# A third weight block, later stores and an earlier gate in a hybrid decoder layer

## The chip, the cores and the metric

The kernel runs on one core of a Trainium2 chip. Its time is device microseconds of one execution, given as the median of several runs. A separate profiled execution supplies the trace that the text reads from.

## The reference, cut to what matters

One layer, 512 tokens of width 2048, all in float32. Two branches read the same normalised input, and their outputs are merged:

```
mod = silu(c) @ w_ada + b_ada;  shift, scale, gate = split(mod, 3)
h = rms_norm(x) * (1 + scale) + shift
proj = h @ w_in                         # all channels of both branches
a_out = swa_attention(...) * silu(ag);  y_a = a_out @ w_o_swa
o = gated_delta_rule(q, k, v, g, beta)  # 16 key heads, 32 value heads
o = rms_norm(o) * silu(dz);             y_b = o @ w_o_dn
y = sigmoid(mg_a) * y_a + sigmoid(mg_b) * y_b
out = x + gate * (y @ w_out)
```

The delta rule works on chunks of 64 tokens. Each chunk needs the inverse of a unit lower triangular 64 x 64 matrix for each head, and then a scan over the chunks carries a state of 128 x 128 per value head. `gate` is a vector of 2048 numbers, the last third of `silu(c) @ w_ada + b_ada`; it is wanted only at the very end.

## The kernel before, in words

**Matmuls.** Each float32 operand is split into a high part (a rounded copy, `whi`, made by ScalarE) and a low part (`wlo`, the difference, made by VectorE); line 50, `split`. A product is three matmuls on TensorE (PE), high by high, high by low, low by high (`mm3`, lines 239 to 244).

**Weights.** All weight matrices are a list of jobs in the order of their use (`plan`, line 158). A job is a block of 128 x 2048 numbers, 1 MB. `load_job` (197) starts its transfer on SyncE's queue (SP) into a tile `raw` of the pool `wraw`, which has two buffers. A block is split in two halves (`split_half`, 206), each into one of three buffers for `whi` and `wlo`. A channel tile (`channel_tile`, 246) takes one block, 48 matmuls of 128 x 512, and gives 128 channels for all tokens. When PE has used a half, `half_done` puts the next split on a list, `due`; when a block's second half has been split, its `raw` buffer is free and the next `load_job` is put there.

**Order.** After every second of a channel tile's 16 steps the kernel calls `pump` (81), so eight times in a tile. A pump first runs the list `due`, then moves all generators in `live` on (a generator says with `yield n` how many pumps it wants to wait), then the paced ones, then those in `side` queues (`beside`, 78), each at a rate of steps per pump. In this way work of the scans, the solves and other helpers is laid between the matmuls. The framework then orders the instructions of each engine by when they are ready and by their place in the program. `ordered` (660) and `behind` (105) add the constraint that a helper's instructions come no earlier than the matmul ahead of them in the program.

**Stages.** The startup computes h; the keys' stage the keys, their matrices and the first of two triangular solves. Then comes the heads' stage, the second half of `deltanet` (593): for each of 16 heads a channel tile of queries, two of values and two of the output gate z (`heads`, 843), two channel tiles of the merge gate behind them. The generators `queries`, `values`, `zgate` and `scan` run beside the tiles of their own head and of the next one. The second solve runs on VectorE until it is drained at head 8; its buffers are the pool `sol1`. From head 2 on `od_sums` (674) builds sums of weight blocks by transfers in DRAM (`od_m`), copies on SP's queue and accumulating ones on GpSimd's.

A scan (953) goes through four chunks. In each, ScalarE copies `vn` from PSUM, VectorE scales it to `vs`, PE multiplies it (`pd`, line 988), and ScalarE puts the outputs into `osb` (993), a single buffer. At the end `osb` is normalised, transposed and multiplied with z, and `head_sums` (1034) forms four sums of quarters and stores everything to DRAM, `oq_d`, with three transfers on SP (1044).

`branch_b` (1047) is the output product of this branch: it loads `oq_d` and multiplies it with the weights `w_od` and the sums (`od`). Beside it, at a rate of 0.17, ran `gate` (1595): it loads `w_ada_gate` in 32 pieces of 512 KB (`gw`, two buffers), adds each times a number of silu(c) to an accumulator `gate_bc` on VectorE (1612, 1614), sums over the partitions with four matmuls against ones (`pgate`, 1622), adds the bias and halves (1624, 1625), and stores the result in `gate_d`. Attention and the last product follow, and are not touched.

Of the kernel before, what the change touches and what calls it, by code (L numbers as in the profile page):

```python
# [7 lines left out]
F32 = mybir.dt.float32  # L8
# [8 lines left out]
P = 128  # L17
# [19 lines left out]
class Layer:  # L37
# [153 lines left out]
    def prime(self):  # L191
        self.job_load = self.half_split = self.half_used = 0
        self.raws, self.halves, self.due = {}, {}, []
        for _ in range(2):
            self.load_job()

    def load_job(self):
        j = self.job_load
        if j < len(self.jobs):
            src = self.jobs[j][1]  # L200
            raw = self.wraw.tile([P, 2048], F32, tag="raw", name="raw")
            self.nc.sync.dma_start(out=raw[:, : src.shape[-1]], in_=src)
            self.raws[j] = raw
            self.job_load += 1

    def split_half(self):
        n = self.half_split
        j = n // 2
        if j < len(self.jobs):
            w = self.jobs[j][1].shape[-1] // 2  # L210
            raw = self.raws[j]
            hi = self.whl.tile([P, 1024], F32R, tag="whi", name="whi")
            lo = self.whl.tile([P, 1024], F32R, tag="wlo", name="wlo")
            self.split(hi[:, :w], lo[:, :w], raw[:, (n % 2) * w : (n % 2 + 1) * w])
            self.halves[n] = (hi, lo)
            self.half_split += 1
            if n % 2:
                del self.raws[j]
                self.due.append(self.load_job)

    def half(self, name):
# [57 lines left out]
    def build(self):  # L279
        tc, nc, a = self.tc, self.nc, self.a  # L280
        with ExitStack() as es:
            self.const = es.enter_context(tc.tile_pool(name="const", bufs=1))
            self.dram = es.enter_context(tc.tile_pool(name="scratch", bufs=1, space=DRAM))
            self.dnc_es = ExitStack()
            self.dnc = self.dnc_es.enter_context(tc.tile_pool(name="dnc", bufs=1, side="right"))
            self.v_d = self.dram.tile([2, P, T], F32, name="v_d")
            self.hpool = es.enter_context(tc.tile_pool(name="h", bufs=1))
            hh = self.hh = self.hpool.tile([P, KT, T], F32R, name="hh")
            hl = self.hl = self.hpool.tile([P, KT, T], F32R, name="hl")
            self.wraw = es.enter_context(tc.tile_pool(name="wraw", bufs=2, reuse_waits="tile"))  # L290
            self.whl = es.enter_context(tc.tile_pool(name="whl", bufs=3, reuse_waits="tile"))
            self.side, self.live, self.slow = {}, [], []
            self.hold, self.keep_order = 0, False
            self.od_d = {n: self.dram.tile([8, P, 2048], F32, name=f"od_{n}") for n in ("m7", "m5", "m6", "m4")}
            self.plan()
            self.psc_es = ExitStack()
            self.psc = self.psc_es.enter_context(tc.tile_pool(name="psc", bufs=4, space=PSUM, reuse_waits="tile"))
            with ExitStack() as st:
                self.startup(st)
            if self.stop == "startup":  # L300
                return
            self.ma_d = self.dram.tile([KT, P, T], F32, name="ma_d")
            self.mb_d = self.dram.tile([KT, P, T], F32, name="mb_d")
            self.ao_d = self.dram.tile([KT, P, T], F32, name="ao_d")
            self.yb_d = self.dram.tile([KT, P, T], F32, name="yb_d")
            self.deltanet()
            self.psc_es.close()
            self.dnc_es.close()
            if self.stop == "deltanet":
                return  # L310
            self.gate_d = self.dram.tile([D], F32, name="gate_d")
            self.y_d = self.dram.tile([KT, P, T], F32, name="y_d")
            self.branch_b()
            if self.stop == "branch_b":
                return
            self.attention()
            if self.stop == "attention":
                return
            self.finish()
# [273 lines left out]
    def deltanet(self):  # L593
# [10 lines left out]
        with ExitStack() as ps:  # L604
            self.pmm = ps.enter_context(tc.tile_pool(name="pmm", bufs=2, space=PSUM, reuse_waits="tile"))
            self.ptp = ps.enter_context(tc.tile_pool(name="ptp", bufs=2, space=PSUM, reuse_waits="tile"))
            self.gwk = ps.enter_context(tc.tile_pool(name="gwk", bufs=1, reuse_waits="tile"))
            sol1 = ps.enter_context(tc.tile_pool(name="sol1", bufs=1, side="right", reuse_waits="tile"))
            with ExitStack() as sa:
                wk = sa.enter_context(tc.tile_pool(name="dnA", bufs=2, reuse_waits="tile"))  # L610
                sol0 = sa.enter_context(tc.tile_pool(name="sol0", bufs=1, reuse_waits="tile"))
# [27 lines left out]
            with ExitStack() as sb:  # L639
                wk = sb.enter_context(tc.tile_pool(name="dnB", bufs=2, reuse_waits="tile"))  # L640
                self.tt = []
                for n in range(4):
                    t = wk.tile([P, NTB, P], F32, tag=f"tt{n}", name=f"tt{n}", bufs=1)
                    nc.gpsimd.memset(t[HD:P, :, 0:HD], 0.0)
                    self.tt.append(t)
                for g in range(KH):
                    if g == 2:
                        self.beside(self.ordered(self.od_sums()), 0.13, "ws")
                    if g == 8:
                        self.drain_slow(s1)  # L650
                    self.heads(wk, g)
                for j in range(3, 5):
                    self.merge_gate("ma", j, self.ma_d)
                self.drain_live()
                self.drain("ws")

    def sum_keys(self):
        return [(s, n, i) for s in ("m7", "m5", "m6", "m4") for n in range(2) for i in range(2)]
# [294 lines left out]
    def scan(self, wk, g, k, kT, TT, qd, M, epsq, st):  # L953
# [73 lines left out]
        for e in range(2):  # L1027
# [1 line left out]
            self.transpose4(pt, lambda c: osb[:, e, c, :])  # L1029
            nc.vector.tensor_tensor(out=z[e], in0=pt, in1=z[e], op=ALU.mult)  # L1030
            yield 1
        self.head_sums(g, z, osb.rearrange("p e c i -> p (e c i)").rearrange("p (q t) -> p q t", q=4))

    def head_sums(self, g, z, s):

        nc = self.nc
        TT, STT = nc.vector.tensor_tensor, nc.vector.scalar_tensor_tensor
        lo, hi = slice(0, 256), slice(256, 512)
        TT(out=s[:, 0], in0=z[0][:, hi], in1=z[1][:, hi], op=ALU.subtract)
        STT(out=s[:, 1], in0=s[:, 0], scalar=-1.0, in1=z[0][:, lo], op0=ALU.mult, op1=ALU.subtract)  # L1040
        TT(out=s[:, 2], in0=z[0][:, lo], in1=z[0][:, hi], op=ALU.add)
        STT(out=s[:, 3], in0=s[:, 1], scalar=-1.0, in1=z[1][:, lo], op0=ALU.mult, op1=ALU.subtract)
        for q, src in ((slice(0, 1), z[0][:, lo].unsqueeze(1)), (slice(1, 3), z[1].rearrange("p (q t) -> p q t", q=2)), (slice(3, 7), s)):
            nc.sync.dma_start(out=self.oq_d[q, g // 2].rearrange("q p k t -> p q k t")[:, :, g % 2, :], in_=src)


    def branch_b(self):
        tc, nc, a = self.tc, self.nc, self.a
        with ExitStack() as es:
# [3 lines left out]
            self.gwk = es.enter_context(tc.tile_pool(name="gwkb", bufs=1, reuse_waits="tile"))  # L1053
            k1 = wk.tile([P, 2, 2, T], F32, name="k1", bufs=1)
            k5 = wk.tile([P, 2, 2, T], F32, name="k5", bufs=1)
            self.beside(self.gate(wk), 0.17, "gate")
            order = self.od_order()
            raws, parts, c = {}, {}, {}

# [42 lines left out]
            for m, (name, _, _) in enumerate(order):  # L1102
                ps = {}
                for kt in range(KT):
# [15 lines left out]
                    self.half_done()  # L1120
                    if kt % 2:
                        del parts[u]
            self.drain("gate")
            for j in range(7, 9):
                self.merge_gate("ma", j, self.ma_d)
            self.drain_live()
# [468 lines left out]
    def gate(self, wk):  # L1595

        nc, a = self.nc, self.a
        acc = wk.tile([P, D], F32, name="gate_bc", bufs=1)
        ws = {}

        def load(i):
            ws[i] = wk.tile([P, 1024], F32, tag="gw", name="gw", bufs=2)
            nc.sync.dma_start(out=ws[i], in_=a["w_ada_gate"][i // 2][:, i % 2 * 1024 : i % 2 * 1024 + 1024])

        load(0)
        load(1)
        for i in range(2 * KT):
            yield
            s = self.sc[:, i // 2 : i // 2 + 1]
            o = acc[:, i % 2 * 1024 : i % 2 * 1024 + 1024]  # L1610
            if i < 2:
                nc.vector.tensor_scalar(out=o, in0=ws.pop(i), scalar1=s, scalar2=None, op0=ALU.mult)
            else:
                nc.vector.scalar_tensor_tensor(out=o, in0=ws.pop(i), scalar=s, in1=o, op0=ALU.mult, op1=ALU.add)
            if i + 2 < 2 * KT:
                load(i + 2)
        for c in range(4):
            sl = slice(c * T, (c + 1) * T)
            b = wk.tile([P, T], F32, tag="yb", name="gb", bufs=3)
            nc.sync.dma_start(out=b, in_=a["b_gate"][sl].partition_broadcast(P))  # L1620
            ps = self.ptp.tile([P, T], F32, tag="tp", name="pgate")
            nc.tensor.matmul(ps, lhsT=self.ones, rhs=acc[:, sl], start=True, stop=True)
            yield
            nc.vector.tensor_tensor(out=acc[:, sl], in0=ps, in1=b, op=ALU.add)
            nc.vector.tensor_scalar(out=acc[:, sl], in0=acc[:, sl], scalar1=0.5, scalar2=None, op0=ALU.mult)
            nc.sync.dma_start(out=self.gate_d[sl], in_=acc[0:1, sl])


# [78 lines left out]
```

## Time and profile before

| | us |
|---|---|
| median of 3 runs | 2908.98 |
| lowest and highest run | 2906.93, 2910.56 |
| profiled execution | 2908.68 |
| its span, first to last instruction | 2906.9 |
| PE busy in the span | 2839.3 |
| VectorE (DVE) busy | 1846.5 |
| ScalarE (ACT) busy | 1141.0 |
| GpSimd (POOL) busy | 270.7 |

The heads' stage lies from about 527 to 1655 us, the output product from there to about 2000. In the profile's lists a line such as `PE pd L988 <- DVE vs L980: 15.7, 6, 6.6` says that PE, at line 988 with output `pd`, waited for `vs` of VectorE: the total, how often, and the longest. In a timeline a line begins with its start and its duration, and ends in brackets with the engine's idle time before it and what ended that.

### The profile page before, as it was taken

What the parts mean: (1) busy time and instruction counts of PE and PEld (TensorE: products, weight loads), DVE (VectorE), ACT (ScalarE), POOL (GpSimd) and SP (SyncE); (2) the same over time, 40 slices, a digit from 0 to 9 for tenths busy, and PEclk for the clock granted to TensorE, in tenths of its full rate; (3) what the DMA queues carried; (4) which work ended last, traced back from release to release, by engine and by line L of the source; (5) the groups of instructions that cost most, each with busy time, mean ns of one, the idle gap of its engine ahead of it and who ended that gap; (6) DMA issues with size and microseconds to landing.
All of it is one profiled execution on the core that took longest, in us unless ns stands there. A gap on an engine that the chain in (4) does not pass through costs nothing. (4 is left out here: it accounts for less than half of the span.)

```text
span 2906.9 us, 38230 instructions
## 1 busy us (share of the span) xinstructions
PE 2839.3 (98%) x14428; PEld 2325.5 (80%) x14428; DVE 1846.5 (64%) x3020; ACT 1141.0 (39%) x2161; POOL 270.7 (9%) x266
## 2 busy tenths in 40 slices
PE   8899999999999999999999999999999999999999
PEld 6677888888887888888878888778887788788777
DVE  6765898777776655545545477765655655554565
ACT  4354333433334333333333355443344434432343
POOL 0022211101111111111110000000100100000010
PEclk9999999999999999999999999999999999999999
DMA  9747454646667767666663499876645647365575
GB/s 388 285 148 212 161 183 144 205 130 202 202 187 217 234 178 220 200 204 188 208 168 121 135 337 327 305 257 207 215 155 162 171 142 223 113 239 177 179 236 153
DMA packets 205472, 590.08 MB, mean 203 GB/s; under 512 B 74564, under 2 KB 99652, under 8 KB 154088
## 3 DMA queue, kind: packets, MB, share of 16 engines
q1 hardware_dynamic: 195080, 529.44, 53.2%
q0 software_dynamic: 10208, 58.20, 10.1%
q8 instruction: 113, 1.85, 0.3%
q14 instruction: 71, 0.58, 0.1%
HBM read 523.79 MB, written 166.40 MB: 237 GB/s over the span
## 5 line engine op out<-in xcount | busy, mean ns | idle before, releaser
L242 PE MATMUL mm<-hh,whi 128*128 128x512 f32 x2784 | 1133.2, 407 | 2.5 <-ACT whi L52 1.6
L244 PE MATMUL mm<-hh,wlo 128*128 128x512 f32 x2784 | 1090.8, 392 | 1.5 <-DVE wlo L53 1.5
L243 PE MATMUL mm<-hl,whi 128*128 128x512 f32 x2784 | 1089.1, 391 | 0.0
L53 DVE TENSOR_TENSOR wlo<-raw,whi 128x1024 fp32r<-128x1024 f32 (+1 forms) x476 | 585.5, 1233 | 457.7 <-ACT whi L52 447.9
L52 ACT CAST whi<-raw 128x1024 fp32r<-128x1024 f32 (+1 forms) x476 | 494.8, 1043 | 815.2 <-PE mm L243 644.9
L244 PEld LDWEIGHTS mm<-hh,wlo 128*128 128x128 f32 x2784 | 523.7, 188 | 116.1 <-DVE wlo L53 2.4
L242 PEld LDWEIGHTS mm<-hh,whi 128*128 128x128 f32 x2784 | 524.9, 189 | 112.7 <-issue 8.6
L243 PEld LDWEIGHTS mm<-hl,whi 128*128 128x128 f32 x2784 | 525.4, 189 | 98.5 <-issue 0.5
L243 PE MATMUL od<-wlo,oh 128*128 128x512 f32 x448 | 175.7, 392 | 3.3 <-DVE wlo L53 3.2
L242 PE MATMUL od<-whi,oh 128*128 128x512 f32 x448 | 176.4, 396 | 0.2 <-ACT whi L52 0.2
L244 PE MATMUL od<-whi,ol 128*128 128x512 f32 x448 | 175.2, 391 | 0.0
L920 POOL TENSOR_TENSOR qe<-qe,yq 128x512 f32<-128x512 f32 x32 | 47.8, 1508 | 884.3 <-DMA qe<-eg_rows 761.3
L769 POOL TENSOR_TENSOR E<-E,neg_g 128x512 f32<-128x512 f32 x64 | 80.0, 1250 | 489.4 <-DMA E<-g_rows 400.3
L819 DVE TENSOR_TENSOR A<-A,atmp 128x62 f32<-128x62 f32 (+30 forms) x124 | 111.4, 898 | 1.5
L812 DVE TENSOR_TENSOR atmp<-A 128x62 f32<-128x62 f32 (+30 forms) x124 | 110.1, 888 | 1.4
L243 PEld LDWEIGHTS od<-wlo,oh 128*128 128x128 f32 x448 | 84.6, 189 | 23.0 <-DVE wlo L53 4.9
L242 PEld LDWEIGHTS od<-whi,oh 128*128 128x128 f32 x448 | 84.4, 188 | 18.6 <-issue 1.0
L244 PEld LDWEIGHTS od<-whi,ol 128*128 128x128 f32 x448 | 84.5, 189 | 17.7
L53 DVE TENSOR_TENSOR wlo<-raww,whi 128x1024 fp32r<-128x1024 f32 x56 | 68.2, 1221 | 41.2 <-ACT whi L52 41.2
L52 ACT CAST whi<-raww 128x1024 fp32r<-128x1024 f32 x56 | 59.0, 1054 | 76.6 <-PE m L244 67.1
L966 DVE SCALAR_TENSOR_TENSOR r<-pp,neg_eg,vt 128x128 f32<-128x128 f32 x96 | 29.2, 346 | 81.0 <-PE pp L963 79.7
L1369 ACT ACTIVATE sm<-sm,mx,rs 128x256 f32<-128x256 f32 (+1 forms) x128 | 71.7, 561 | 3.3 <-DVE mx L1364 3.3
(341 smaller groups left out, 3254.2 us busy)
## 6 DMA issues: line engine op xcount, KB each, us to landing
raw<-in_w_ch SPq DMA_DIRECT2D x158, 1024.0 KB
wa<-in_w_ada_ss SPq DMA_DIRECT2D x32, 1024.0 KB
od_m<-in_w_od POOLq DMA_DIRECT2D x32, 1024.0 KB, 14.1
raw<-od_m SPq DMA_DIRECT2D x32, 1024.0 KB
raw<-in_w_od SPq DMA_DIRECT2D x24, 1024.0 KB
E<-g_rows SPq DMA_DIRECT2D x64, 256.0 KB
od_m<-in_w_od SPq DMA_DIRECT2D x16, 1024.0 KB
od_m<-od_m SPq DMA_DIRECT2D x16, 1024.0 KB
```

The costliest lines, as they stand in the source:

```text
L52: self.nc.scalar.copy(out=hi, in_=src)
L53: self.nc.vector.tensor_tensor(out=lo, in0=src, in1=hi.bitcast(F32), op=ALU.subtract)
L242: nc.tensor.matmul(ps, lhsT=wh, rhs=xh, start=first, stop=False)
L243: nc.tensor.matmul(ps, lhsT=wh, rhs=xl, start=False, stop=False)
L244: self.last_mm = nc.tensor.matmul(ps, lhsT=wl, rhs=xh, start=False, stop=last).ins
L769: nc.gpsimd.tensor_tensor(out=E, in0=E, in1=ng, op=ALU.add)
L812: eng.tensor_tensor(out=t, in0=A[:, m : m + 1, m + 1 :].to_broadcast([P, m, n]), in1=A[:, :m, m : m + 1].to_broadcast([P, m, n]), op=ALU.mult,
L819: eng.tensor_tensor(out=A[:, :m, m + 1 :], in0=A[:, :m, m + 1 :], in1=t, op=ALU.add)
L920: nc.gpsimd.tensor_tensor(out=qf, in0=qf, in1=q, op=ALU.mult)
L966: nc.vector.scalar_tensor_tensor(out=r[:, e, :], in0=pp[:, e, :], scalar=self.neg_eg[:, c, 2 * g + e : 2 * g + e + 1], in1=v[e][:, c, :], ...
L1369: nc.scalar.activation(t, t, AF.Exp, scale=r[:, h : h + 1], bias=mx[:, h : h + 1], accum_out=den[:, h : h + 1])
```

## The change

Three edits.

1. **A third weight block.** In the heads' stage a pool `wmore` gives one more buffer for `raw`, and one `load_job` more is called at the stage's start. From then on three blocks are on their way or waiting instead of two. `load_job` takes the buffer that is free, in `wraw` or in `wmore`. With the last head `wmore` is set to None, so that the extra block is used up and not loaded again.
2. **Stores.** `head_sums` becomes a generator that waits four pumps between its sums and its three stores.
3. **The gate.** It runs no longer in `branch_b` but from head 8 of the heads' stage on, in a pool `late` in the place of the second solve's `sol1`, at a rate of 0.125, under `ordered`. Its bias tile has a buffer of its own. A `yield` is added between the eviction of each of the four sums and its store. `gate_d` is made earlier, since it is written earlier.

```diff
     def load_job(self):
         j = self.job_load
-        if j < len(self.jobs):
+        pool = self.wmore if sum(p is self.wraw for p in self.raw_in.values()) == 2 else self.wraw
+        if j < len(self.jobs) and pool:
             src = self.jobs[j][1]
-            raw = self.wraw.tile([P, 2048], F32, tag="raw", name="raw")
+            raw = pool.tile([P, 2048], F32, tag="raw", name="raw")
+            self.raw_in[j] = pool
...
             if n % 2:
-                del self.raws[j]
+                del self.raws[j], self.raw_in[j]
                 self.due.append(self.load_job)
...
+                self.wmore = sb.enter_context(tc.tile_pool(name="wmore", bufs=1, reuse_waits="tile"))
+                self.load_job()
                 for g in range(KH):
+                    if g == KH - 1:
+                        self.wmore = None
...
                     if g == 8:
                         self.drain_slow(s1)
+                        es1.close()
+                        late = ps.enter_context(tc.tile_pool(name="late", bufs=1, side="right", reuse_waits="tile"))
+                        self.beside(self.ordered(self.gate(late)), 0.125, "gate")
...
                 self.drain("ws")
+                self.drain("gate")
...
         STT(out=s[:, 3], in0=s[:, 1], scalar=-1.0, in1=z[1][:, lo], op0=ALU.mult, op1=ALU.subtract)
+        yield 4
         for q, src in ((slice(0, 1), z[0][:, lo].unsqueeze(1)), (slice(1, 3), z[1].rearrange("p (q t) -> p q t", q=2)), (slice(3, 7), s)):
             nc.sync.dma_start(out=self.oq_d[q, g // 2].rearrange("q p k t -> p q k t")[:, :, g % 2, :], in_=src)
...
-            self.beside(self.gate(wk), 0.17, "gate")
...
-            self.drain("gate")
...
             nc.tensor.matmul(ps, lhsT=self.ones, rhs=acc[:, sl], start=True, stop=True)
             yield
             nc.vector.tensor_tensor(out=acc[:, sl], in0=ps, in1=b, op=ALU.add)
             nc.vector.tensor_scalar(out=acc[:, sl], in0=acc[:, sl], scalar1=0.5, scalar2=None, op0=ALU.mult)
+            yield
             nc.sync.dma_start(out=self.gate_d[sl], in_=acc[0:1, sl])
```

More of the change, by code (lines that the diff above doesn't have):

```diff
@@ L193, in prime @@
         self.raws, self.halves, self.due = {}, {}, []
+        self.raw_in, self.wmore = {}, None
         for _ in range(2):
@@ L305, in build @@
             self.yb_d = self.dram.tile([KT, P, T], F32, name="yb_d")
+            self.gate_d = self.dram.tile([D], F32, name="gate_d")
             self.deltanet()
@@ L310, in build @@
                 return
-            self.gate_d = self.dram.tile([D], F32, name="gate_d")
             self.y_d = self.dram.tile([KT, P, T], F32, name="y_d")
@@ L607, in deltanet @@
             self.gwk = ps.enter_context(tc.tile_pool(name="gwk", bufs=1, reuse_waits="tile"))
-            sol1 = ps.enter_context(tc.tile_pool(name="sol1", bufs=1, side="right", reuse_waits="tile"))
+            es1 = ExitStack()
+            sol1 = es1.enter_context(tc.tile_pool(name="sol1", bufs=1, side="right", reuse_waits="tile"))
             with ExitStack() as sa:
@@ L1031, in scan @@
             yield 1
-        self.head_sums(g, z, osb.rearrange("p e c i -> p (e c i)").rearrange("p (q t) -> p q t", q=4))
+        yield from self.head_sums(g, z, osb.rearrange("p e c i -> p (e c i)").rearrange("p (q t) -> p q t", q=4))
     def head_sums(self, g, z, s):
@@ L1618, in gate @@
             sl = slice(c * T, (c + 1) * T)
-            b = wk.tile([P, T], F32, tag="yb", name="gb", bufs=3)
+            b = wk.tile([P, T], F32, tag="gb", name="gb", bufs=1)
             nc.sync.dma_start(out=b, in_=a["b_gate"][sl].partition_broadcast(P))
```

## The prediction, made before the result was known

> **What bounds the kernel now.** I read the page first, then the chain of waits engine by engine (PE alone, by stage), then the busy times of stretches around each stall, and last the timeline of the longest stall.
>
> ```profile
> span 2906.9 us, 38230 instructions
> PE 2839.3 (98%) x14428; PEld 2325.5 (80%) x14428; DVE 1846.5 (64%) x3020; ACT 1141.0 (39%) x2161; POOL 270.7 (9%) x266
> ```
>
> TensorE is busy 2839.3 of 2906.9 us, so an edit that leaves the matmuls alone can only win from the other 67.6 us and from time at a lower clock. The change touches two stages, the heads' stage (527 to 1655 us) and the output product behind it (1655 to about 2000). PE's waits in the first, and in the second:
>
> ```profile
> PE pd L988 <- DVE vs L980: 15.7, 6, 6.6
> PE pto L276 <- DVE osb L1023: 1.3, 1, 1.3
> PE pv L973 <- ACT vt L870: 1.1, 1, 1.1
> PE ptv L276 <- DVE yv L590: 0.7, 1, 0.7
> ```
>
> ```profile
> PE od L243 <- DVE wlo L53: 3.2, 2, 2.2
> ```
>
> One wait is nearly all of it: `pd`, a matmul of the scan, waits for `vs` on VectorE six times, 15.7 us in all. Around these stalls the clock drops as well (columns: stretch, its length, busy time of PE, PEld, DVE, ACT and POOL with instruction counts, granted clock, DMA share, GB/s):
>
> ```profile
> 918.00:928.00 10.00, 6.62 (x24) 5.40 (x24) 5.25 (x12) 7.58 (x14) 0.00 (x0) 0.83 0.79 247
> 1260.00:1270.00 10.00, 8.01 (x37) 6.38 (x36) 4.39 (x8) 4.34 (x10) 0.00 (x0) 1.00 0.94 313
> 1330.00:1342.00 12.00, 9.65 (x37) 7.66 (x37) 4.38 (x8) 4.34 (x10) 0.00 (x0) 0.86 0.94 302
> 1487.50:1494.00 6.50, 6.50 (x25) 5.62 (x25) 1.14 (x3) 1.35 (x6) 0.00 (x0) 0.67 0.00 0
> 1852.00:1864.00 12.00, 9.77 (x36) 7.62 (x35) 11.57 (x14) 4.65 (x5) 0.00 (x0) 0.86 0.86 315
> ```
>
> Clock lost is length times (1 - granted): 1.7 us at 918, 1.7 at 1330, 2.1 behind the stall that ended at 1487.5, 1.7 at 1852; none at 1260. That is 5.5 us in the heads' stage and 1.7 in the output product.
>
> Why `vs` is late is told by the longest stall (start, duration, engine, line, operation, idle time before it and who ended it):
>
> ```profile
> 1460.89 12.44 SPq L202 DMA_DIRECT2D raw<-in_w_ch  x2
> 1484.74 1.04 ACT L52 CAST whi<-raw 128x1024 fp32r<-128x1024 f32 x1 [11.93 <-DMA raw<-in_w_ch]
> 1485.69 0.37 ACT L975 COPY vn<-pv 128x256 f32<-128x256 f32 x1
> 1485.82 1.23 DVE L53 TENSOR_TENSOR wlo<-raw,whi 128x1024 fp32r<-128x1024 f32 x1 [10.23 <-ACT whi L52]
> 1486.96 0.48 DVE L980 TENSOR_SCALAR vs<-vn,kd 128x128 f32<-128x128 f32 x2
> 1487.49 1.22 PE L988 MATMUL pd<-vs,k 128*128 128x256 f32 x2 [6.60 <-DVE vs L980]
> ```
>
> ScalarE stands 11.93 us at the split of a weight block that was asked for at 1460.89 and came 23.9 us later. The scan's `vn` is queued behind that split, VectorE's `wlo` and `vs` behind it too, and PE waits at `pd`. The reader is to see that a weight load nobody on PE needs yet holds two in-order engines. It happens seven times:
>
> ```profile
> L52 ACT CAST whi<-raw x164: 1030/1047/1067, 531.3 to 1648.8; 128x1024 fp32r<-128x1024 f32 x164
>   DMA raw<-in_w_ch: 41.1, 7
> ```
>
> ```profile
> L692 POOL DMA_DIRECT2D od_m<-in_w_od x32: 819/1114/2060, 694.1 to 1453.1; - x32
> 1450.92 4.19 POOL L692 DMA_DIRECT2D od_m<-in_w_od  x5
> DMA to landing us min/median/max: 8.1/14.1/28.5
> ```
>
> The second fence says what is ahead of such a load: GpSimd issues five accumulating 1 MB transfers in a row just before (its last ones, by the first line); these take 8.1 to 28.5 us to land.
>
> **The third weight buffer.** A load is issued when a block's second half has been split, and that moment does not move. What moves is which block it fetches: one later than before. 164 half splits from 531.3 to 1648.8 us are 6.86 us each, so a block lasts 13.7 us and every load gets 13.7 us more. The longest ACT wait is 11.93, so without anything new in the queue all seven are covered, the worst with 1.8 us to spare. Gone with them: 15.7 us of stalls and 5.5 us of clock. No instruction is added; one 1 MB load goes out earlier at the stage's start. I cost it at nothing: the address it fills lies, by my sum of the pools' sizes, beyond the previous stage's buffers, and DMA share there is two thirds (first row below). If it does wait for old buffers it holds SP, and loads behind it have as much cover as today. In the last head the third buffer is given up again; the od_sums transfers are over by then and DMA share is half (third row).
>
> ```profile
> 527.00:1067.00 540.00, 534.12 (x2798) 442.56 (x2797) 384.90 (x639) 204.30 (x439) 70.46 (x66) 1.00 0.66 198
> 1067.00:1345.00 278.00, 272.91 (x1432) 226.20 (x1431) 144.33 (x269) 101.23 (x228) 35.45 (x35) 0.99 0.69 202
> 1500.00:1650.00 150.00, 148.99 (x786) 123.90 (x784) 76.72 (x153) 55.20 (x126) 9.87 (x8) 1.00 0.34 110
> 1650.00:1960.00 310.00, 306.20 (x1357) 250.75 (x1358) 227.40 (x244) 144.41 (x170) 0.00 (x0) 0.99 0.85 303
> ```
>
> **The gate's sums, moved.** What is carried from 1650-1960 to heads 8 to 15 (all instructions on its accumulator, one row; then its common operation; then its loads):
>
> ```profile
> 1650.00:1960.00 310.00, 4.09 (x8) 1.44 (x8) 44.22 (x40) 0.99 0.85 303
> L1614 DVE SCALAR_TENSOR_TENSOR gate_bc<-gw,silu_c,gate_bc x30: 1277/1279/1284, 1675.7 to 1884.5; 128x1024 f32<-128x1024 f32 x30
> gw<-in_w_ada_gate SPq DMA_DIRECT2D x32, 512.0 KB
> ```
>
> Where it leaves: VectorE falls from 227.4 to 183 of 310 us, and 16.8 MB of 94 go. The two PE stalls there (3.2 us) and their clock (1.7) are late splits as well; I take both as gone, with 0 as the other end. The 4.1 us on PE only move.
>
> Where it arrives: at a rate of 0.125 one step comes every eight pumps, so at the end of each channel tile, 13.7 us apart. VectorE in the second half is busy 52% (144.3 of 278); 44.2 us more over some 570 make 60%, under the 71% (384.9 of 540) of the first half, where the second solve runs beside the scans. So the load is no issue and the place is:
>
> ```profile
> 1134.61 1.23 DVE L53 TENSOR_TENSOR wlo<-raw,whi 128x1024 fp32r<-128x1024 f32 x1 [3.01 <-ACT whi L52]
> 1135.76 0.47 DVE L980 TENSOR_SCALAR vs<-vn,kd 128x128 f32<-128x128 f32 x2
> 1136.75 0.60 PE L988 MATMUL pd<-vs,k 128*128 128x256 f32 x2
> ```
>
> Here a tile ended at 1133.5 and VectorE was idle 3.01 us before `wlo`: the sum fits there. If it were put right ahead of `vs`, it would cost 1.28 less the 0.52 us between the end of `vs` (1136.23) and `pd`: 0.76 us, once a head, 6.1 us over eight. I take 0, nearest to the idle row.
>
> Its loads: 202 GB/s at a share of 0.69 is 293 GB/s at full share, so 512 KB cost 1.8 us, five a head 9 us of 68.6 (five blocks): share 0.82. One or two ahead of a late block eat 1.8 to 3.6 us of cover, which leaves the worst block up to 1.8 us late; seven ACT waits gave six PE waits, so a short one can cost nothing. I take 0. On SP a gate load waits for its sum on VectorE (1.3 us and what is before it); raw loads behind it have their 13.7 us. Its four matmuls each hold one of the stage's two transpose banks for a step (13.7 us), since the eviction comes a step later; the scans' transposes then share the other. No row shows that; the nearest are the waits at transposes, 0.7 and 1.3 us. Bounds 0 to 4 x 1.3 = 5.2; I take 1, because the banks are needed in pairs only once a head.
>
> **The stores, four pumps later.**
>
> ```profile
> SPq L1044 <- DVE zh L1030: 133.0, 29, 9.5
> ACT osb L993 <- DMA oq_d<-osb: 0.9, 2, 0.7
> ```
>
> SP stands 133 us in front of these stores, with raw loads behind it; freeing it is worth nothing on PE beyond the raw waits already counted. Later stores have a price: the scan's result buffer is single, and in two heads ScalarE already waits for the store. How far the scheduler really moves them I can't see: it orders by readiness as well as by place in the program. Bounds: 0, and one stall like the longest one, 6.6 + 2.1 = 8.7 us, at the head whose store would fall behind the five transfers. I take 0.
>
> **Sum.** 15.7 + 5.5 + 3.2 + 1.7 - 1 = 25.1 us off the profiled execution of 2908.7 us, which is 0.3 us under the median of the runs (2909.0): 2884 us.
>
> A rule against one term: the Trainium skill ("TensorE: Matmul & The Clock Gate", section "HAM oscillation — how this bites in real kernels") says PE gaps beyond about 3.4 us drop the clock to half. By it the stalls at 918 (3.38), 1330 (2.35) and 1852 (2.23) would cost no clock, and the sum would be 5.1 us smaller, 2889. This trace disagrees: clock was lost in all three, and not at 1260 (1.99).
>
> **The rivals.**
>
> The store takes the wait over: ScalarE stands at `osb` behind a late store, once or more. For it: the two waits above; against it: they were 0.7 us at most. 2884 + 8.7 = 2893.
>
> The sums fall ahead of `vs`: 2884 + 6.1 = 2890. Against it: the idle row.
>
> GpSimd is held:
>
> ```profile
> L920 POOL TENSOR_TENSOR qe<-qe,yq x32: 1277/1300/2292, 550.5 to 1584.7; 128x512 f32<-128x512 f32 x32
> ACT E L914 <- POOL E L770: 78.6, 28, 7.1
> 985.94 0.63 ACT L914 ACTIVATE E<-E 128x512 f32<-128x512 f32 x1 [7.06 <-POOL E L770]
> 988.20 0.57 ACT L870 COPY vt<-ptv 128x512 f32<-128x512 f32 x1
> ```
>
> The same operation on GpSimd takes 1.28 us or up to 2.29, so something beside it can cost it 1.0 us, and ScalarE already waits 78.6 us for GpSimd's masks; the longest of these waits stands ahead of the `vt` for which PE waited 1.1 at `pv`. If each of eight heads loses 1.1, that is 8.8: 2893. The Trainium skill ("SBUF — State Buffer", section "Who interferes with whom") gives the reason a VectorE instruction with two SBUF inputs, as the gate's sum, contends with a GpSimd one that reads SBUF; the row agrees that something does.
>
> Slower: DMA becomes the bound in heads 8 to 13. A head leaves (1 - 0.69) x 68.6 = 21.3 us of DMA time. At 1.8 us a gate load takes 9 of them; at 4.3 it takes all; at 5.2 (26 us, 4.7 over, for the 5.6 heads until 1453) the gain is gone. At half of the median landing of a 1 MB accumulate, 7 us, it is 14 over, 78 us: 2962. Against it: the last stage row moved 303 GB/s with these same loads, at a share of 0.85, and PE hardly waited.
>
> The buffer does nothing: the loads land later by as much as they are wanted later, because something ahead of them in the queue also moves. Then only the output product gains its 4.9: 2904.
>
> **How the numbers follow.** 0.2% is 5.8 us, about what a measurement of this kernel can tell from no change. Forecast 0.60; store 0.12; sums ahead of `vs` 0.07; GpSimd 0.04; DMA-bound 0.11; no effect 0.06. Faster is the first four, 0.83; same 0.06; slower 0.11. The likeliest case's own range is 2878 (the other 3.1 us of waits in the heads' stage and the 1 for the banks go too, and the runs shown lie up to 2 us under their median) to 2889 (no gain in the output product). With two of the dearer bounds at once, 8.7 at the store and 8.8 at the masks, it reaches 2901, which leaves out the last two cases, 0.17.
>
> **What would show it.** Right: ScalarE's waits for `raw` in the heads' stage go from 41.1 us to under 5, `pd <- vs` from 15.7 to under 2, no clock under 1.0 from 900 to 1650, the gate's sums at tile ends from about 1090 to 1530, the output product's DMA share down to about 0.8. Wrong: a new wait at `osb` for its store, `pd <- vs` of 0.8 us once a head, ScalarE's wait for the masks up, DMA share near 1 from 1090 on with `raw` still waited for.

## The result, and the profile after

The changed kernel takes 2912.36 us (median of 20 runs, 2902.22 to 2914.88), the kernel before 2908.95 us (median of 20 runs, 2905.57 to 2913.53). The ratio is 1.0009, with a 95% interval of 1.0002 to 1.0016: 0.1% slower, which is less than the 0.2% that the prediction took as the least that can be told from no change. Forecast were 2884 us and a range of 2878 to 2901.

The first profiled execution was the shortest of its 20 runs (2902.22 us). The rows below are therefore of a second one, of 2914.90 us, unless a sentence says otherwise. First the head of its page:

```profile
span 2913.1 us, 38269 instructions
PE 2844.6 (98%) x14428; PEld 2330.6 (80%) x14428; DVE 1859.3 (64%) x3020; ACT 1139.5 (39%) x2161; POOL 270.8 (9%) x266
```

PE's waits in the heads' stage (527 to 1665 us; total, times, longest):

```profile
PE ptv L279 <- DVE yv L593: 17.1, 7, 4.0
PE pd L1000 <- DVE vs L992: 2.7, 1, 2.7
PE pto L279 <- DVE zh L1042: 2.2, 1, 2.2
PE pto L279 <- DVE osb L1035: 1.3, 1, 1.3
PE pv L985 <- ACT vt L882: 1.3, 1, 1.3
```

The old wait, `pd` for `vs`, has gone from 15.7 us to 2.7. ScalarE's waits for `raw` in this stage have no row any more (41.1 us before). In their place stands a new wait of the same size: `ptv`, the transposes of a value tile, wait for the finished value tile `yv`. One of its seven, 0.72 us at 624.64, stood in the kernel before too. The other six lie in heads 9 to 14, one a head. Three of them, and the granted clock around each (columns as in the prediction):

```profile
1172.70 0.63 PE L279 MATMUL ptv<-ident,yv 128*128 128x128 f32 x4 [2.96 <-DVE yv L593]
1243.66 0.30 PE L279 MATMUL ptv<-ident,yv 128*128 128x128 f32 x1 [1.86 <-DVE yv L593]
1315.08 0.45 PE L279 MATMUL ptv<-ident,yv 128*128 128x128 f32 x1 [3.96 <-DVE yv L593]
```

```profile
1167.00:1179.00 12.00, 9.04 (x40) 7.42 (x39) 8.98 (x13) 4.95 (x7) 3.31 (x4) 0.86 0.96 241
1239.00:1249.00 10.00, 8.14 (x43) 6.58 (x41) 8.91 (x13) 4.96 (x7) 4.14 (x6) 1.00 0.73 158
1312.00:1322.00 10.00, 6.92 (x25) 6.06 (x26) 6.70 (x10) 3.49 (x5) 1.61 (x2) 0.66 0.94 218
```

Clock is lost behind the longer two, 12 x 0.14 = 1.7 us at 1167 and 10 x 0.34 = 3.4 at 1312, and none behind the shortest. Over the whole heads' stage the trace's clock records add up to 12.0 us lost; in the kernel before they add up to 6.8 (the prediction's three stretches hold 5.5 of it; the other 1.3 fall inside the longest stall, where PE stands anyway).

The gate's sums are where they were expected, and the output product is relieved about as expected, VectorE to 190 us where 183 were forecast (VectorE's sums; ScalarE's wait for the masks in the heads' stage; the stretch that the prediction shows; PE's wait there):

```profile
L1625 DVE SCALAR_TENSOR_TENSOR gate_bc<-gw,silu_c,gate_bc x30: 1266/1277/2323, 1115.4 to 1530.0; 128x1024 f32<-128x1024 f32 x30
ACT E L926 <- POOL E L782: 90.5, 26, 7.3
1650.00:1960.00 310.00, 307.63 (x1383) 254.21 (x1382) 189.92 (x215) 146.83 (x183) 0.00 (x0) 1.00 0.70 243
PE od L246 <- DVE wlo L53: 1.0, 1, 1.0
```

**Where the new wait comes from.** The stall at 1172.70, as ScalarE and then VectorE saw it:

```profile
1167.00 0.63 ACT L926 ACTIVATE E<-E 128x512 f32<-128x512 f32 x1 [5.92 <-POOL E L782]
1168.79 0.63 ACT L926 ACTIVATE E<-E 128x512 f32<-128x512 f32 x1 [1.16 <-POOL E L782]
1169.33 1.03 ACT L52 CAST whi<-raw 128x1024 fp32r<-128x1024 f32 x1
1170.26 0.62 ACT L591 ACTIVATE th<-yv 128x512 f32<-128x512 f32 x1
```

```profile
1159.38 0.69 DVE L1035 TENSOR_TENSOR osb<-osb,roy 128x512 f32<-128x512 f32 x1
1159.99 1.28 DVE L1625 SCALAR_TENSOR_TENSOR gate_bc<-gw,silu_c,gate_bc 128x1024 f32<-128x1024 f32 x1
...
1161.79 1.25 DVE L900 TENSOR_SCALAR epsq<-ss 128x4 f32<-128x4 f32 x1
...
1166.53 0.73 DVE L586 SCALAR_TENSOR_TENSOR yv<-mm,convh,yv 128x509 f32<-128x509 f32 x1
...
1170.39 1.22 DVE L53 TENSOR_TENSOR wlo<-raw,whi 128x1024 fp32r<-128x1024 f32 x1 [1.53 <-ACT whi L52]
...
1171.87 0.68 DVE L593 SCALAR_TENSOR_TENSOR yv<-th,yv 128x512 f32<-128x512 f32 x1
```

And VectorE at the same place in the kernel before:

```profile
1162.10 1.29 DVE L1023 TENSOR_TENSOR osb<-osb,roy 128x512 f32<-128x512 f32 x2
1163.32 0.16 DVE L888 TENSOR_SCALAR epsq<-ss 128x4 f32<-128x4 f32 x1
1164.52 2.31 DVE L583 SCALAR_TENSOR_TENSOR yv<-mm,convh,yv 128x511 f32<-128x511 f32 x3
```

Two things have changed. First, a gate sum now lies between the two `osb` normalisations at the end of a scan, and the three convolution steps of the value tile behind it end later: 7.9 us after the first `osb` starts (1159.38 to 1167.26), where it was 4.7 (1162.10 to 1166.83). Second, ScalarE has another order: the tanh `th` of the value tile stands behind both mask exponentials `E`, which wait for GpSimd, and behind a weight split; before, it stood behind one exponential. The convolution was done at 1167.26, and `th` starts at 1170.26, 3.0 us later. PE waited 2.96.

The framework writes down an order for each engine when the kernel is built, so that orders can be compared without a run; in the profiles ScalarE ran in the order of this table. It goes from the first value tile's first step `yv` to its copy `vt`, in heads 9 to 14:

```
head  before              changed             sums mid-tile (e3)  sums at pump 2 (e7)
 9    yv E th E whi vt    yv E E whi th vt    yv E th E whi vt    yv E E whi th vt
10    yv E th whi E vt    yv E whi th E vt    yv E th whi E vt    yv E whi th E vt
11    yv E th E whi vt    yv E E whi th vt    yv E th E whi vt    yv E E whi th vt
12    yv th E E whi vt    yv E E whi th vt    yv th E E whi vt    yv E E whi th vt
13    yv th whi E E vt    yv whi th E vt      yv th whi E E vt    yv whi th E E vt
14    yv E th E whi vt    yv E E whi th vt    yv E th E whi vt    yv E E th whi vt
```

The profiles of the other kernels fall in line with it: the gate moved alone has the order of the changed kernel in all six heads; the gate left in the output product, the buffer alone and the stores alone have the order of the kernel before.

### The profile page after: what moved, and what is told of

It is laid out like the page before. It is cut to its first block, busy times and chain, and to the rows that moved or that the text cites. A ratio compares the mean times of both kernels' runs of the same rounds, so it can differ in the third digit from the quotient of the medians.

```text
span 2900.5 us, 38269 instructions
## 1 busy us (share of the span) xinstructions
PE 2833.8 (98%) x14428; PEld 2322.5 (80%) x14428; DVE 1863.0 (64%) x3020; ACT 1141.2 (39%) x2161; POOL 273.9 (9%) x266
## 4 chain that ended last, share of the span: by engine, by line
PE 81%; issue 4%; DVE 4%; DMA 2%; POOL 1%; ACT 1%; SPq 0%; POOLq 0%; DVEq 0%; ACTq 0%
PE mm L245 19%; PE mm L247 18%; PE mm L246 18%; PE od L245 4%; PE od L246 4%; PE od L247 4%; PE m L246 1%; PE m L247 1%; PE m L245 1%; PE S L1356 1%; PE pv L985 1%; PE O L1407 1%; PE po L1004 1%; PE pP L279 1%; DVE wlo L53 1%
## 5 line engine op out<-in xcount | busy, mean ns | idle before, releaser
L245 PEld LDWEIGHTS od<-whi,oh 128*128 128x128 f32 x448 | 84.1, 188 | 17.1
L246 PEld LDWEIGHTS od<-wlo,oh 128*128 128x128 f32 x448 | 84.1, 188 | 17.1
L53 DVE TENSOR_TENSOR wlo<-raww,whi 128x1024 fp32r<-128x1024 f32 x56 | 68.3, 1222 | 41.1 <-ACT whi L52 41.1
```

The costliest lines, as they stand in the source:

```text
L53: self.nc.vector.tensor_tensor(out=lo, in0=src, in1=hi.bitcast(F32), op=ALU.subtract)
L245: nc.tensor.matmul(ps, lhsT=wh, rhs=xh, start=first, stop=False)
L246: nc.tensor.matmul(ps, lhsT=wh, rhs=xl, start=False, stop=False)
```

## The experiments

The theory ("order theory" in the expectations): where a gate sum stands decides the order that is written for ScalarE and VectorE around it; at the end of a tile the tanh falls behind the exponentials and a split, and PE waits for it. The rivals: the waits were chance, or they come from the third buffer or the stores, from the time of the sums alone, or from their loads. Each ratio is against the kernel before as it ran in the same session (medians 2906.57 to 2909.85 us).

**The changed kernel again.**

> The changed kernel once more, unaltered, for a profile of a usual execution. Theory (order on ScalarE): a gate sum lies inside the chain that ends a scan on VectorE, and the planner puts ScalarE's tanh of the first value tile behind both mask exponentials and a weight split; TensorE then waits at the transposes ptv for yv, 14 to 20 us in 6 to 8 waits, in heads 9 to 14, in every execution, and time 2908 to 2915. Rival (chance): these waits belong to the one profiled execution; then they differ here by more than 5 us, or lie in other heads.

Measured 2914.83 us (2907.51 to 2916.49, 11 runs), ratio 1.0018 (1.0008 to 1.0027). The waits are those shown above; in the first profile the same six heads waited (15.7 us in 7). They aren't chance. What differs most between the two profiled executions is the clock, as the last section shows.

**The gate back in the output product.**

```diff
-                        self.beside(self.ordered(self.gate(late)), 0.125, "gate")
...
+            self.beside(self.gate(wk), 0.17, "gate")
             order = self.od_order()
...
```

> The changed kernel with the gate's sums back in the output product; the third weight buffer and the later stores stay. Order theory: the tanh comes before the exponentials again, ptv <- yv under 3 us, raw still not waited for; 2908.7 - 15.7 - 5.5 = 2888, 2884 to 2892. Rival (buffer or stores): weight splits that are ready earlier push the tanh back; then ptv <- yv stays over 10 us and the time is 2905 to 2918.

2891.40 us, ratio 0.9944 (0.9931 to 0.9958). PE's wait at `ptv` in the heads' stage:

```profile
PE ptv L279 <- DVE yv L593: 2.0, 3, 0.9
```

The new wait needs the gate; the buffer and the stores don't bring it.

**The sums in the middle of a tile.** The rate counter starts at a half, so that each step comes at the fourth of a tile's eight pumps.

```diff
                         self.beside(self.ordered(self.gate(late)), 0.125, "gate")
+                        self.side["gate"][0][2] = 0.5
```

> The changed kernel with the gate's steps four pumps earlier, in the middle of each channel tile; same loads, same sums, same number of steps. Order theory: the tanh keeps its place, ptv <- yv under 3 us, 2880 to 2890. Rival (load): 44 us of sums on VectorE, or their 32 loads of 512 KB, slow the heads wherever they stand; then PE's waits in heads 8 to 14 stay over 12 us, at ptv or elsewhere, and the time is 2903 to 2915.

2886.97 us, ratio 0.9931 (0.9918 to 0.9945): faster than both kernels, with the same sums, loads and buffers as the changed one. PE's waits in the heads' stage:

```profile
PE pd L1001 <- DVE vs L993: 3.2, 2, 2.6
...
PE ptv L279 <- DVE yv L593: 0.7, 1, 0.7
```

ScalarE and VectorE at the place where the changed kernel stalled first (`ptv` at 1167.87, no wait):

```profile
1164.73 0.63 ACT L927 ACTIVATE E<-E 128x512 f32<-128x512 f32 x1 [5.36 <-POOL E L783]
1165.26 0.62 ACT L591 ACTIVATE th<-yv 128x512 f32<-128x512 f32 x1
```

```profile
1165.91 1.05 DVE L593 SCALAR_TENSOR_TENSOR yv<-th,yv 128x512 f32<-128x512 f32 x1 [2.92 <-ACT th L591]
1166.88 1.27 DVE L1626 SCALAR_TENSOR_TENSOR gate_bc<-gw,silu_c,gate_bc 128x1024 f32<-128x1024 f32 x1
```

The tanh starts at once behind the first exponential, as in the kernel before, and the sum runs just behind the product that PE needs. The load on VectorE and on DMA isn't the cause.

**The gate alone.** The changed kernel without its other two edits: two weight buffers, stores at once.

```diff
-                self.wmore = sb.enter_context(tc.tile_pool(name="wmore", bufs=1, reuse_waits="tile"))
-                self.load_job()
...
-        yield 4
...
```

> The kernel before with the gate's sums moved alone: two weight buffers, stores at once. Order theory: the ptv waits come up as in the changed kernel (12 to 16 us in 6 to 8 waits) beside most of the old waits at pd for vs; against before less 4.9 in the output product, plus 15 us of waits and some 5 of clock: 2915 to 2927. Rival (buffer or stores cause the waits): no ptv waits, 2904.

2923.32 us, ratio 1.0051 (1.0035 to 1.0066). Both waits stand beside each other:

```profile
PE pd L996 <- DVE vs L988: 14.4, 6, 7.9
PE ptv L279 <- DVE yv L593: 14.4, 7, 3.0
```

So the changed kernel is a gain and a loss of like size, not a change without effect.

**The tanh put first, the sums left at the tile's end.** The exponentials are ordered behind the tanh of the first value tile; the helper `after_tanh`, left out here, adds that constraint and no wait.

```diff
...
-        for e in range(2):
-            nc.scalar.activation(M[e], M[e], AF.Exp)
+        with self.after_tanh():
+            for e in range(2):
+                nc.scalar.activation(M[e], M[e], AF.Exp)
```

> The changed kernel, sums where they are, but both mask exponentials of a head are ordered behind the tanh of its first value tile on ScalarE (order alone, no wait). In heads 9 to 14 one weight split (1.03 us) still stands ahead of that tanh. Order theory: ptv <- yv falls from 17.1 to under 6 us, 2885 to 2897. Rival (the sum's own 1.28 us on VectorE inside the scan's end delays yv): the sums have not moved, so 12 us or more of waits stay, 2905 to 2916.

2897.13 us, ratio 0.9961 (0.9949 to 0.9973), and

```profile
PE ptv L293 <- DVE yv L609: 7.8, 5, 2.5
```

That is more than the 6 us of the order theory and far less than the 12 of its rival; the time is 0.1 us above the theory's range. What is left is told by the longest wait, 2.52 us at 1240.20 (ScalarE, then VectorE):

```profile
1236.15 0.63 ACT L605 ACTIVATE th<-yv 128x512 f32<-128x512 f32 x1 [2.17 <-DVE yv L600]
```

```profile
1227.93 1.28 DVE L1643 SCALAR_TENSOR_TENSOR gate_bc<-gw,silu_c,gate_bc 128x1024 f32<-128x1024 f32 x1
...
1237.90 1.21 DVE L53 TENSOR_TENSOR wlo<-raw,whi 128x1024 fp32r<-128x1024 f32 x1
...
1239.37 0.68 DVE L609 SCALAR_TENSOR_TENSOR yv<-th,yv 128x512 f32<-128x512 f32 x1
```

The tanh now starts as soon as the convolution is done and ends at 1236.78, but the product on VectorE comes 2.6 us later, behind four instructions written ahead of it. So with the tanh ahead of the exponentials, 7.8 us are left of the 16.4 that heads 9 to 14 waited in the changed kernel. What is left lies on VectorE: in all six heads the product starts 1.4 to 2.6 us after the tanh ended, with VectorE busy in between. A longer chain and an order of its own stand there; how these two share the 7.8 us was not separated. In head 10 the wait even grew, from 1.86 us to the 2.52 shown.

**Short sums.** Each sum over 64 of its 1024 columns, all loads whole; the kernel leaves out the rest of the gate's sums, and sets its accumulator to zero first:

```diff
...
-            o = acc[:, i % 2 * 1024 : i % 2 * 1024 + 1024]
+            o = acc[:, i % 2 * 1024 : i % 2 * 1024 + 64]
...
```

> The changed kernel, its 32 gate steps at the same places with the same 512 KB loads, but each sum over 64 of its 1024 columns (the rest of the gate's sums is left out). Order theory: with the short sums the planner puts no split and at most one exponential ahead of the tanh in heads 9 to 13, both exponentials in 14; ptv <- yv under 4 us, 2880 to 2891. Rival (the loads, on their queue and on DMA, make the masks late): 12 us or more of waits stay, 2903 to 2915.

2890.18 us, ratio 0.9937 (0.9925 to 0.9949):

```profile
PE ptv L279 <- DVE yv L593: 0.9, 2, 0.7
```

The 32 loads at the tile's end cost PE nothing at `ptv`. It is the length of the sum there. With the short sums the tanh also stands ahead of the split in all six heads, so that this run doesn't part the length from the order.

**The sums at the second pump** of a tile, in the program far from the scan's end.

```diff
                         self.beside(self.ordered(self.gate(late)), 0.125, "gate")
+                        self.side["gate"][0][2] = 0.75
```

> The changed kernel with the gate's steps at the second of a tile's eight pumps instead of the eighth, far from the end of a scan. Order theory: the planner again puts both exponentials and a split ahead of the tanh in heads 9, 11 and 12, one and a split in 10 and 13, both exponentials alone in 14: ptv <- yv 10 to 18 us, 2902 to 2914. Rival (any place off the scan's end is as good as the middle of a tile): under 4 us, 2887.

2907.19 us, ratio 0.9992 (0.9983 to 1.0001), and

```profile
PE ptv L279 <- DVE yv L593: 13.8, 7, 3.0
```

The written order had the tanh behind the split in heads 9 to 13 (the table above). There PE waited 1.25 to 3.00 us at `ptv`; in head 14, where it stood ahead of the split, PE didn't wait for `yv`. But as VectorE ran it, this place isn't far from the value tile: in all six heads the sum stands between the first two steps of the first value tile's convolution, here in head 9:

```profile
1161.82 1.66 DVE L1626 SCALAR_TENSOR_TENSOR gate_bc<-gw,silu_c,gate_bc 128x1024 f32<-128x1024 f32 x1
1164.66 0.73 DVE L586 SCALAR_TENSOR_TENSOR yv<-mm,convh,yv 128x509 f32<-128x509 f32 x1
1169.78 1.23 DVE L53 TENSOR_TENSOR wlo<-raw,whi 128x1024 fp32r<-128x1024 f32 x1 [3.25 <-ACT whi L52]
```

So the two bad places have one thing in common: the sum lies on VectorE ahead of the end of this convolution and makes it later. The delay itself isn't what PE waits for here: the convolution was done at 1165.39, ScalarE ran the tanh only at 1169.65, behind both exponentials and the split, and VectorE stood idle for 3.25 us meanwhile. That a later convolution is what makes the scheduler put the tanh last is an inference; no run shows its reckoning. At the sixth pump (0.25 in place of 0.75) it was the other way:

> The changed kernel with the gate's steps at the sixth of a tile's eight pumps. As planned, the tanh stands ahead of both exponentials and the split in heads 10, 11 and 13, ahead of one exponential and the split in 9 and 12, behind one exponential in 14. Order theory: ptv <- yv under 4 us, 2883 to 2891. Rival (any place nearer the scan's end than the middle loses): 8 us or more of ptv waits, 2896 to 2910.

2889.07 us, ratio 0.9933 (0.9920 to 0.9946), with 0.7 us at `ptv`. Both times the written order told which it would be.

**The buffer alone, the stores alone,** each on the kernel before:

```diff
+                self.wmore = sb.enter_context(tc.tile_pool(name="wmore", bufs=1, reuse_waits="tile"))
+                self.load_job()
...
```

```diff
+        yield 4
         for q, src in ((slice(0, 1), z[0][:, lo].unsqueeze(1)), (slice(1, 3), z[1].rearrange("p (q t) -> p q t", q=2)), (slice(3, 7), s)):
```

> The kernel before with the third weight buffer alone: stores at once, gate in the output product. If the buffer is the gain: 15.7 us of waits at pd for vs fall to under 4 and about 5 us of clock come back, 2885 to 2893. Rival (the later stores are needed too, since they stand ahead of the raw loads on the queue): raw is still waited for, 2895 to 2908.

> The kernel before with the later stores alone (four pumps), two weight buffers, gate in the output product. Prediction's step (stores worth 0): within 4 us of before, pd <- vs still 13 to 18 us in 5 to 7 waits. Rival (they free the queue for raw loads): raw waited for less than before's 41.1 us by half, 2895 to 2903. Rival (they hold the scan's result buffer): ScalarE waits at osb for oq_d over 5 us, 2912 to 2918.

The buffer: 2889.90 us, ratio 0.9936 (0.9923 to 0.9949). The stores: 2908.40 us, ratio 1.0002 (0.9992 to 1.0011). The waits at `pd` with the buffer, then with the stores:

```profile
PE pd L997 <- DVE vs L989: 2.7, 1, 2.7
```

```profile
PE pd L993 <- DVE vs L985: 16.0, 6, 6.5
```

The buffer is nearly all of the gain; the later stores are worth nothing.

**The middle of a tile, with the stores at once.**

```diff
-        yield 4
         for q, src in ((slice(0, 1), z[0][:, lo].unsqueeze(1)), (slice(1, 3), z[1].rearrange("p (q t) -> p q t", q=2)), (slice(3, 7), s)):
```

> The kernel with the sums in the middle of a tile, and the stores issued at once as in the kernel before. If the later stores are worth nothing there either: 2884 to 2891, the same as with them (2887). If they matter beside the gate's loads on the same queue: over 2893, with raw waited for again.

2889.71 us, ratio 0.9939 (0.9925 to 0.9953), against 0.9931 (0.9918 to 0.9945) with the later stores: not told apart. In the profile one store is late, and PE feels it. The later stores have that wait as well (6.11 us at 1467.20 in the profile of the sums in the middle of a tile, where `pd` then waited 0.61 us):

```profile
1471.29 0.37 ACT L1006 COPY osb<-po 128x256 f32<-128x256 f32 x1 [7.61 <-DMA oq_d<-osb]
1474.97 0.48 PE L1001 MATMUL pd<-vs,k 128*128 128x256 f32 x1 [2.11 <-DVE vs L993]
```

ScalarE stands 7.61 us at `osb`, `vn` is queued behind it, and `pd` waits 2.11 us for `vs`. `raw` is not waited for.

## Why the prediction was wrong

The forecast was 25.1 us of gain. The gain is there; a loss of the same size that was taken as 0 stands against it.

- **The step that failed** is "Where it arrives", which put the gate's sums into an idle row of VectorE (`wlo`, 3.01 us idle at 1134.61) and took 0, with 6.1 us as the worst; measured are 16.4 us of new waits at `ptv` in heads 9 to 14, and the clock lost behind four of the six. That row is one tile end of five in a head. At another, the end of a scan, VectorE has no such gap, and the wait is not at `vs`, where the bound was made, but at `ptv`. The price was reckoned as the sum's own 1.28 us less a slack. What moving the sum brought was another order, written for two other chains: the tanh fell behind two exponentials and a split, the product behind a split's `wlo`. The prediction noted that the scheduler orders by readiness, for the stores, and did not apply it to the sums.
- **Its size.** Predicted was a span of 2906.9 - 25.1 = 2881.8 us, with 3.1 + 1.0 us of PE waits and no lost clock in the heads' stage. Found are 24.6 us of waits (the five rows above), which is 20.5 more; 12.0 of clock, 1.1 of it inside the stalls; and 1.0 in the output product: 2881.8 + 20.5 + 10.9 + 1.0 = 2914.2, where 2913.1 were measured. Clock is a third of the miss.
- **The third buffer** was right as a mechanism and in size: 15.7 + 5.5 = 21.2 us forecast, 0.64% of 2909.85 = 18.6 us measured (14.8 to 22.4). What stayed is the stall at 918, which the prediction counted among those of `raw`. In the sums-mid-tile kernel it is another one:

```profile
923.86 2.12 ACT L837 COPY atmp<-A 64x512 f32<-64x512 f32 x2 [5.85 <-DMA ta_d<-atmp]
```

  ScalarE stands 5.85 us at a copy of the second solve that waits for its own earlier store, with the split and `vn` queued behind it. Before, a wait for `raw` stood in that place.
- **The gate out of the output product** was right: waits 3.2 to 1.0 us, clock 1.00, DMA share 0.85 to 0.70, below the 0.8 forecast. With the sums in the middle of a tile the whole kernel gains 0.69%, 20.1 us of the 25.1 forecast; that is another kernel than the one forecast. Against the gate left in the output product (2891.40) the intervals overlap, so that the move's own worth, some 4 us by the medians, is not shown.
- **The banks,** 1 us taken: a wait of 2.2 us at 1599.34, `pto` for `zh`, which no kernel with the gate in the output product has, and 1.7 us of clock behind it. One, not four. A product of the gate stood in its bank from 1590.20 until VectorE took it at 1603.14, across this wait; but in the kernel with the gate moved alone one stood so as well (1599.56 to 1610.46), and `pto` at 1606.65 stood 0.11 us. That the bank caused the wait is argued, not shown.
- **The loads and the stores** at 0 were right (short sums; stores alone). The mechanism of the stores' rival didn't come about in the changed kernel (0.8 and 1.1 us at the longest in its two profiles). It exists where the sums stand in the middle of a tile, with later and with early stores alike: waits of 6.11 and 7.61 us at `osb`, behind which PE waited 0.61 and 2.11 us; behind the second 1.7 us of clock were lost too. The rival of a held GpSimd had its sign, 78.6 to 90.5 us, not its place: the masks come late in every kernel here, and what matters is what stands behind them on ScalarE.
- **The rival of the slower side** was looked for in DMA. The one that came about, a reordering on an engine that the edit doesn't touch, was not among the rivals. "No effect" had a chance of 0.06, for a buffer that does nothing; that the time hardly changed came of a gain and a loss that happen to be of one size.

## What to carry to other kernels

An instruction put into an in-order engine's program can cost more than its duration less the idle time: a scheduler that orders by readiness may write another order for its neighbours, on other engines too. Before judging such an edit by busy shares, compare the written orders before and after around the places where PE's operands are made, and look at what stands in front of them that waits for something else. The place within the tile then is a knob: against the kernel before, the same 32 sums gave a ratio of 1.0018 at the eighth pump, 0.9992 at the second, 0.9933 at the sixth and 0.9931 at the fourth.

## What the runs showed of the hardware

**Short stalls cost clock, and not always.** In the heads' stage and the output product, the shortest stall with lost clock is 2.10 us (the kernel with mid-tile sums and early stores):

```profile
929.54 0.48 PE L1001 MATMUL pd<-vs,k 128*128 128x256 f32 x1 [2.10 <-DVE vs L993]
925.00:935.00 10.00, 7.90 (x32) 6.44 (x31) 2.83 (x6) 8.12 (x14) 0.00 (x0) 0.83 0.48 125
```

The one of 1.86 us above lost none, and one of 2.98 in the first profile of the changed kernel lost none either:

```profile
1310.50 0.30 PE L279 MATMUL ptv<-ident,yv 128*128 128x128 f32 x1 [2.98 <-DVE yv L593]
1308.00:1318.00 10.00, 7.50 (x52) 6.19 (x53) 8.68 (x13) 2.92 (x5) 1.04 (x2) 1.00 1.01 227
```

So in these stages it is open between about 2 and 3 us whether a stall costs 1.7 us more. That is most of the difference between two executions of the changed kernel: its two profiled ones have 15.7 and 17.1 us at `ptv`, but 5.1 and 12.0 us of lost clock in the heads' stage, together 8.3 of the 12.6 us between their spans. In the startup, where stalls follow each other closely, the clock also fell behind shorter ones: in the kernel before behind one of 1.32 us at 264.64, to 0.54 from 266.3 to 270. The Trainium skill ("TensorE: Matmul & The Clock Gate", section "HAM oscillation — how this bites in real kernels") puts the gap from which the clock falls at about 3.4 us; these rows disagree.

**VectorE beside GpSimd.** An `epsq` of 128 x 4 takes 0.16 us in the kernel before and 1.25 in the changed one, at 1161.79, where GpSimd is at work:

```profile
1161.30 2.97 POOL L932 TENSOR_TENSOR qe<-qe,yq 128x512 f32<-128x512 f32 x2 [53.04 <-DVE gate_bc L1625]
```

In the kernel before the same pair of products began after `epsq`:

```profile
1164.03 2.98 POOL L920 TENSOR_TENSOR qe<-qe,yq 128x512 f32<-128x512 f32 x2 [54.02 <-DMA qe<-eg_rows]
```

By moving VectorE's chain the sum brought the two together, which adds 1.1 us to the chain that is late. It isn't this one instruction alone: of VectorE's 480 instructions of 128 x 4 or 128 x 8, those that took over 0.6 us (10 in the kernel before, 16 in the changed one) all ran while GpSimd was at work, and of the others only 20 and 25 did.
